# Small tiles of a two-block transformer kernel moved into its pool of constants; scratch of the squares in bfloat16

## The chip, the core and the metric

The kernel runs on one core of one Trainium2 chip, in one launch. The metric is the device time in microseconds (us). A profile is one execution of its own, taken by the hardware profiler; its span runs from the first to the last instruction.

## What is computed

Two transformer blocks act on x of 256 tokens by 1024 features, all in float32:

```
def first_block(x, ...):
    h = _swiglu(_rms_norm(x, ffn1_pre_norm), ffn1_w_in, ffn1_w_out)          # 1024 -> 2 x 2816 -> 1024
    x = x + 0.5 * _rms_norm(h, ffn1_post_norm)
    m = _token_mixing(_rms_norm(x, mix_pre_norm), w_mix_in, ...)             # retention + neighbourhood attention
    x = x + _rms_norm(m, mix_post_norm)
    h = _swiglu(_rms_norm(x, ffn2_pre_norm), ffn2_w_in, ffn2_w_out)
    return x + 0.5 * _rms_norm(h, ffn2_post_norm)

def second_block(x, c, ...):
    mod = silu(c) @ ada_w + ada_b                                            # 2 x 6 x 1024 modulations
    for i in range(2):
        h = x * (1 + scale1) + shift1
        y = moba_attention(h, ...) if i == 0 else diff_attention(h, ...)
        x = layer_norm(sqrt(2) * x + (1 + gate1) * y, ln_g[i, 0], ln_b[i, 0])
        h = x * (1 + scale2) + shift2
        y = square(relu(h @ mlp_w_up[i])) @ mlp_w_down[i]                    # 1024 -> 4096 -> 1024
        x = layer_norm(sqrt(2) * x + (1 + gate2) * y, ln_g[i, 1], ln_b[i, 1])
    return x
```

## The kernel before

**Precision.** Every large product is made of three matmuls in the type fp32r. A weight tile `raw` (128 x 1024, float32) is rounded by ScalarE to `wh` (L115), and VectorE subtracts to get the rest `wl` (L93). Activations are kept the same way as a high and a low part, side by side in one tile (`XX`, `H`, `Y`, `N`). A product is high by high, low by high and high by low. In `mmA` (512 columns) the activation is the stationary operand and the weight moves; in `mmB` (256 columns) the weight is stationary and `XX` moves. This text calls the three matmuls of one call of `mmA` or `mmB` a triple. In the profile's names the moving operand comes first: `acc<-wh,H` moves `wh` past a stationary slice of `H`.

```
    def mmA(o, wh, wl, x, s, e):
        mm(o, x[:, 0], wh, s, False)
        mm(o, x[:, 0], wl, False, False)
        mm(o, x[:, 1], wh, False, e)
```

**Stages.** The first SwiGLU (`swiglu`, 11 slices of 256 hidden features), mixing, the second SwiGLU, then twice an attention and an MLP (`mlp`, 16 slices). `XX` holds the normalised, transposed input of a stage. `H` (four to five buffers) holds a slice of the hidden layer, and `down` and `down_tail` multiply it by the second weight matrix: 8 triples a slice. `Y` holds the merged heads: in mixing it is multiplied by `w_ret_out` (`yr`, 32 triples) and `w_mix_out` (`acc`, 32), in each attention by its output matrix (`oacc`, 32). `N` holds the heads of the neighbourhood attention (`yn`, 16 triples).

**Order of the work.** The order is written out by hand: `tick` brings in weight pieces up to a look-ahead (rings of 6 `raw` buffers and 8 of `wh` and `wl`) and runs side tasks. The modulations `ada` are summed on VectorE into `adacc` (L335, L338), split into three bfloat16 parts by ScalarE and GpSimd (L348 to L354) and multiplied on TensorE at set places.

**Where tiles lie.** A pool lays its tiles one behind the other in each partition, in the order of first use, each rounded up to a multiple of 32 bytes. The pools stand in the order const, wts, big, work, and behind them the pools of the stage at hand (hid, mix, att0, att1, ada, late). Tiles of a few bytes a partition (`s`, `r`, `sa`, `bs`, `mv` and the like: sums of squares, their roots, means) are in work, and in mix and att0/att1 (`nmx`, `m3`, `mx`, `ss`, `rs` and the like). The const pool has an odd number of blocks of 32 bytes behind `small`, and so has the work pool with its 29 small blocks. Adding up gives these starts, in bytes of the partition:

| tile | pool | start before | modulo 64 |
|---|---|---|---|
| `raw`, `wh`, `wl` | wts | 24128, 48704, 81472 and multiples of 4096 on | 0 |
| `X`, `XX`, `N` and `v`, `adacc`, `T` and `vt` | big | 114240, 122432, 138816, 147008, 151104 | 0 |
| `junk`, `a`, `b`, `q`, `hf` and the like (512 columns) | work | 159360, 161792 and multiples of 2048 on | 0 |
| `H` | hid | 180704 and multiples of 4096 on | 32 |
| `Y` | mix, att0, att1 | 176608, 186848 | 32 |
| `nv`, `bias`, `cosr`, `sinr`, `R` | mix | 192992 to 211424 | 32 |
| `q`, `k` of the attentions | att0, att1 | 203232 to 209376 | 32 |
| `ada0` to `ada2`, `grow`, `prow`, `lng`, `lnb` | ada, late, hid | 170464 to 192992 | 32 |
| `rq`, `rk`, `dec`, `nP`, `nT`, `P`, `T`, `o` | mix, att0, att1 | 211712 to 228096 | 0 |
| `identb`, `cmaskb`; `sm`, `adb`, `mod`, `csil` | const | 21888, 22144; 22432 to 23712 | 0; 32 |

The slices that TensorE loads start at multiples of 512 bytes within `XX`, `N`, `Y`, `H`, `wh` and `wl`.

The change touches the body of `block_kernel`, the helpers `rpow`, `rcol` and `squares`, the classes `PostRms`, `PostLn` and `Rms`, `log_sigmoid`, and the allocations in `mixing` and `attention`; all matmuls are recorded at L201 (`mm`).

Of the kernel before, what the change touches and what calls it, by code (L numbers as in the profile page):

```python
# [9 lines left out]
F32 = mybir.dt.float32  # L10
F32R = mybir.dt.float32r
BF16 = mybir.dt.bfloat16
AF = mybir.ActivationFunctionType
# [158 lines left out]
def block_kernel(ctx, tc, A, out):  # L172
    nc = tc.nc
    V, SC, PE, GP = nc.vector, nc.scalar, nc.tensor, nc.gpsimd

    const = ctx.enter_context(tc.tile_pool(name="const", bufs=1))
    wpool = ctx.enter_context(tc.tile_pool(name="wts", bufs=1))
    big = ctx.enter_context(tc.tile_pool(name="big", bufs=1))
    work = ctx.enter_context(tc.tile_pool(name="work", bufs=1))
# [45 lines left out]

    ident = cst[:, C_ID:C_ID + 128]
    identb = const.tile([128, 128], BF16, name="identb")
    cmaskb = const.tile([128, 128], BF16, name="cmaskb")
    small = const.tile([128, 4], F32, name="small")
    ones, mhalf, onesb = small[:, 0:1], small[:, 1:3], small[:, 3:4].bitcast(BF16)[:, 0:1]  # L230
# [316 lines left out]


    def rpow(s):
        r = work.tile([128, 2], F32, name="r", bufs=6)[:, 0:s.shape[1]]  # L550
        GP.tensor_tensor(r, s, mhalf[:, 0:s.shape[1]], OP.pow)
        return r

    def rcol(p, c, n, eps):
        s = work.tile([128, 2], F32, name="s", bufs=4)[:, 0:p.shape[1]]
        V.tensor_scalar(s, p, c / n, c * eps, op0=OP.mult, op1=OP.add)
        return rpow(s)

# [20 lines left out]

    def squares(s, src):  # L580

        SC.activation(work.tile([128, 512], F32, name="junk"), src, AF.Square, accum_out=s)

    def turn_of(src, a, c, alloc=gu):

# [24 lines left out]
    class PostRms:  # L610
# [2 lines left out]

        def __init__(self, accs, gain, coef, eps):
            self.accs, self.gain, self.coef, self.eps = accs, gain, coef, eps
            self.s = work.tile([128, 2, 2], F32, name="sa", bufs=2)
            self.m = {}

        def bank(self, t, f, ahead=nothing):
# [13 lines left out]
    class PostLn:  # L633
# [3 lines left out]
        def __init__(self, accs, gate):  # L637
            self.accs, self.gate = accs, gate
            self.v = big.tile([128, 2, D], F32, name="v", tag="P2")
            self.s = work.tile([128, 2, 2, 6], F32, name="bs")  # L640
            self.mv = work.tile([128, 2, 2], F32, name="mv", bufs=2)

        def bank(self, t, f, ahead=nothing):
            ahead(3)
            v = half(self.v[:, t], f)
            V.tensor_tensor(v, self.accs[t][f], half(self.gate, f), OP.mult)  # L646
            V.scalar_tensor_tensor(v, half(X[:, t], f), ALPHA, v, op0=OP.mult, op1=OP.add)  # L647
            V.bn_stats(self.s[:, t, f], v)  # L648
            if f:
                V.bn_aggr(self.mv[:, t], self.s[:, t].rearrange("p f s -> p (f s)"))  # L650
                e = work.tile([128, 1], F32, name="ve", bufs=2)
                V.tensor_scalar(e, self.mv[:, t, 1:2], 0.0, LN_EPS, op0=OP.max, op1=OP.add)  # L652
                self.norm(t, self.mv[:, t, 0:1], rpow(e))

        def norm(self, t, mu, r):
            n = work.tile([128, 1], F32, name="nm", bufs=2)
            V.scalar_tensor_tensor(n, mu, -1.0, r, op0=OP.mult, op1=OP.mult)
            SC.activation(half(self.v[:, t], 0), half(self.v[:, t], 0), AF.Identity, scale=r, bias=n)
            V.tensor_scalar(half(self.v[:, t], 1), half(self.v[:, t], 1), mu, r, op0=OP.subtract, op1=OP.mult)
# [22 lines left out]
    class Rms:  # L682


        def __init__(self):
            self.s = work.tile([128, 2, 2], F32, name="s2", bufs=2)

        def token(self, t):
            for f in range(2):
                squares(self.s[:, t, f:f + 1], half(X[:, t], f))  # L690

        def close(self, c=1.0):
            s = work.tile([128, 2], F32, name="s3", bufs=2)
            V.tensor_tensor(s, self.s[:, :, 0], self.s[:, :, 1], OP.add)
            self.r = rcol(s, c, D, RMS_EPS)

# [103 lines left out]

    def log_sigmoid():
        x = bro[:, 0:8]
        a = work.tile([128, 8], F32, name="ls_a")
        e = work.tile([128, 8], F32, name="ls_e")
        s = work.tile([128, 8], F32, name="ls_s")
        z = work.tile([128, 8], F32, name="ls_z")
        V.scalar_tensor_tensor(a, x, -1.0, x, op0=OP.mult, op1=OP.max)
        yield 1
        SC.activation(e, a, AF.Exp, scale=-1.0)
        yield 1  # L810
        V.tensor_scalar(s, e, 2.0, None, op0=OP.add)
        V.reciprocal(s, s)
        V.tensor_tensor(s, s, e, OP.mult)
        V.tensor_tensor(z, s, s, OP.mult)
        V.memset(a, 1.0 / 21)
        for i in range(9, -1, -1):
            V.tensor_tensor(a, a, z, OP.mult)
            V.tensor_scalar(a, a, 1.0 / (2 * i + 1), None, op0=OP.add)
# [110 lines left out]
    def mixing(mid):  # L929
        with tc.tile_pool(name="mix", bufs=1) as mp:  # L930
# [21 lines left out]
            cosr = mp.tile([128, S], F32, name="cosr")  # L952
            sinr = mp.tile([128, S], F32, name="sinr")
            R = mp.tile([128, S], F32, name="R")
            rh = mp.tile([128, 2], F32, name="rh")
            sgs = {}
            vdone, nvdone = set(), set()

# [10 lines left out]
            def ret_head(h, q, k):  # L969
                hc = h % 2  # L970
                df, e = w2("df"), w2("de")
                GP.iota(two(df), pattern=[[-128, 2], [1, S]], base=0, channel_multiplier=-1,
                        allow_small_or_imprecise_dtypes=True)
                V.tensor_scalar(e, df, lgd[:, h:h + 1], None, op0=OP.mult)
                V.scalar_tensor_tensor(e, df, lgd[:, 4 + h:5 + h], e, op0=OP.mult, op1=OP.min)
                dec = m2("dec")
                SC.activation(dec, e, AF.Exp)
                yield 1
                p = acc("rs")
                for m in range(2):  # L980
                    mm(two(p)[:, m], two(k)[:, hc, m * 128:(m + 1) * 128], two(q)[:, hc], m == 0, True)
                V.scalar_tensor_tensor(dec, p, 128.0 ** -0.5, dec, op0=OP.mult, op1=OP.mult)
                yield 2
                while h not in vdone:
                    yield 1
                p = acc("ry")
                s = mp.tile([128, 2], F32, name="rys", bufs=2)
                for t in range(2):
                    for m in range(2):
                        mm(two(p)[:, t], two(dec)[:, m, t * 128:(t + 1) * 128], rv[:, m, h * 256:(h + 1) * 256],  # L990
                           t == 0 and m == 0, m == 1)
                sq = w2("rsq")
                for t in range(2):
                    SC.activation(two(sq)[:, t], two(p)[:, t], AF.Square, accum_out=s[:, t:t + 1])
                yield 1
                r = rcol(s, 4.0, 256, RMS_EPS)
                yield 1
                V.tensor_tensor(r, r, rms.r, OP.mult)
                while h not in sgs:
                    yield 1  # L1000
                g = sgs.pop(h)
                y = m2("ry")
                for t in range(2):
                    V.scalar_tensor_tensor(two(y)[:, t], two(p)[:, t], r[:, t:t + 1], g[t], op0=OP.mult, op1=OP.mult)
                yield 1
                for v in range(2):
                    for t in range(2):
                        PE.transpose(two(p)[:, v, t * 128:(t + 1) * 128], two(y)[:, t, v * 128:(v + 1) * 128], ident)
                split(Y[:, 2 * h:2 * h + 2, 0], Y[:, 2 * h:2 * h + 2, 1], two(p))

            def na_pair(j, q, k):
                cc = j % 2
                P = [m2("nP"), m2("nP")]
                ps = [acc("ns"), acc("ns")]
                mx = mp.tile([128, 4], F32, name="nmx", bufs=2)
                ss = mp.tile([128, 4], F32, name="nss", bufs=2)
                for c in range(2):
                    for a in range(2):
                        hs = slice(64 * a, 64 * a + 64)
# [1 line left out]
                for a in range(2):  # L1021
                    p = ps[a]
# [192 lines left out]
    def attention(l, turn, after, mid):  # L1215
        with tc.tile_pool(name=f"att{l}", bufs=1) as mp:
# [12 lines left out]

            def pair(j, q, k):  # L1230
                cc = j % 2
                m3 = mp.tile([128, 2, 3], F32, name="m3", bufs=2)
                mx = mp.tile([128, 2, 2], F32, name="mx", bufs=3)
                ss = mp.tile([128, 2, 2], F32, name="ss", bufs=4)
                yield from room(2)
                ps = [acc("as"), acc("as")]
                live[0] += 2
# [20 lines left out]
                if l == 0:  # L1258
                    V.reciprocal(ss, ss)
                else:  # L1260
                    rs = mp.tile([128, 2], F32, name="rs", bufs=4)
                    lr = mp.tile([128, 2], F32, name="lr", bufs=2)
                    V.reciprocal(lr, ss[:, :, 1])
                    V.reciprocal(rs, ss[:, :, 0])
                    V.scalar_tensor_tensor(lr, lr, lam[:, 1:2], ss[:, :, 0], op0=OP.mult, op1=OP.mult)
# [37 lines left out]
                                    two(p)[:, :, 0:128].rearrange("p c (a d) -> p c a d", a=2),  # L1303
                                    ss[:, :, :, None].to_broadcast([128, 2, 2, 64]), OP.mult)
                else:
                    sa = mp.tile([128, 2], F32, name="sa", bufs=2)
                    for c in range(2):
                        SC.activation(two(o)[:, c], two(p)[:, c, 0:128], AF.Square, scale=rs[:, c:c + 1],
                                      accum_out=sa[:, c:c + 1])
# [174 lines left out]
```

## Time and profile before

| | |
|---|---|
| median of 3 runs | 1317.36 us (1317.07 to 1321.57) |
| the profiled execution, its own time | 1319.84 us |
| its span | 1318.0 us |
| TensorE busy | 1258.1 us, 95% |
| VectorE, ScalarE, GpSimd busy | 932.2, 642.8, 94.6 us |
| mean granted TensorE clock | 0.983 of 2.4 GHz |
| read from HBM | 269.37 MB |

The time of a matmul in the profile is from its first column in to its last result out, and matmuls overlap: what one costs in a row of them is the distance from its start to the next one's start, which the timeline shows.

### The profile page before, as it was taken

How to read it: one execution, taken by the hardware profiler on the slowest of the kernel's cores; microseconds unless marked ns; L12 is line 12 of the kernel's file. 1: busy time of each engine (PE TensorE's matmuls, PEld its weight loads, DVE VectorE, ACT ScalarE, POOL GpSimd, SP SyncE). 2: the span in 40 equal slices, each digit the busy share in tenths (PEclk: the TensorE clock that was granted, in tenths of full speed). 3: DMA queues.
4: the chain of work that ended last, by engine and by line, in shares of the span. 5: the costliest groups of instructions: out<-in, count | busy, mean ns of one | idle time of the engine just before them, and what ended most of it. 6: DMA issues, size and time to landing. Idle time of an engine off the chain costs nothing. (4 is left out here: it accounts for less than half of the span.)

```text
span 1318.0 us, 18965 instructions
## 1 busy us (share of the span) xinstructions
PE 1258.1 (95%) x7217; PEld 1073.1 (81%) x7222; DVE 932.2 (71%) x1276; ACT 642.8 (49%) x1032; POOL 94.6 (7%) x69
## 2 busy tenths in 40 slices
PE   9999899999999999999999999999899889999996
PEld 7877677888888878778789978988878777899885
DVE  5687576888676677667577667768677976775655
ACT  6543355545454454445455544435444544643540
POOL 0010010222000001001000000101100001000100
PEclk9999999999999999999999999999999999999998
DMA  9778687866576477878554336877665333576650
GB/s 305 258 250 278 212 258 168 261 212 193 190 223 205 145 249 236 290 258 266 171 181 137 112 118 215 266 256 262 221 231 176 113 109 126 175 249 222 223 192 32
DMA packets 167884, 271.68 MB, mean 206 GB/s; under 512 B 15888, under 2 KB 119664, under 8 KB 167792
## 3 DMA queue, kind: packets, MB, share of 16 engines
q1 hardware_dynamic: 161328, 268.36, 62.9%
q10 hardware_dynamic: 6464, 2.10, 1.0%
q8 instruction: 57, 0.93, 0.3%
q14 instruction: 35, 0.29, 0.1%
HBM read 269.37 MB, written 1.05 MB: 205 GB/s over the span
## 5 line engine op out<-in xcount | busy, mean ns | idle before, releaser
L93 DVE TENSOR_TENSOR wl<-raw,wh 128x1024 fp32r<-128x1024 f32 x392 | 487.9, 1273 | 58.2 <-ACT wh L115 57.0
L115 ACT ACTIVATE wh<-raw 128x1024 fp32r<-128x1024 f32 x392 | 399.7, 1055 | 161.7 <-issue 29.2
L201 PE MATMUL acc<-wh,H 128*128 128x512 f32 x864 | 286.5, 399 | 1.5 <-ACT wh L115 1.5
L201 PE MATMUL g<-wh,XX 128*128 128x512 f32 x832 | 268.3, 397 | 2.0 <-DVE XX L596 1.6
L201 PEld LDWEIGHTS acc<-wh,H 128*128 128x128 f32 x864 | 163.7, 189 | 43.2 <-issue 3.0
L201 PEld LDWEIGHTS g<-wh,XX 128*128 128x128 f32 x832 | 158.4, 190 | 37.5 <-DVE XX L596 2.0
L201 PE MATMUL acc<-wl,H 128*128 128x512 f32 x432 | 173.2, 401 | 1.5 <-DVE wl L93 1.5
L201 PE MATMUL g<-wl,XX 128*128 128x512 f32 x416 | 164.6, 396 | 5.2 <-DVE wl L93 5.2
L201 PE MATMUL u<-XX,wh 128*128 128x256 f32 x896 | 163.9, 284 | 1.5 <-ACT wh L115 1.5
L201 PEld LDWEIGHTS u<-XX,wh 128*128 128x128 f32 x896 | 142.2, 193 | 4.2 <-ACT wh L115 1.9
L201 PE MATMUL u<-XX,wl 128*128 128x256 f32 x448 | 127.5, 285 | 2.9 <-DVE wl L93 2.9
L338 DVE SCALAR_TENSOR_TENSOR adacc<-raw,csil,adacc 128x1024 f32<-128x1024 f32 x84 | 107.4, 1279 | 0.8
L201 PEld LDWEIGHTS g<-wl,XX 128*128 128x128 f32 x416 | 79.3, 191 | 23.2 <-DVE wl L93 7.1
L201 PEld LDWEIGHTS acc<-wl,H 128*128 128x128 f32 x432 | 82.0, 190 | 19.2 <-DVE wl L93 2.1
L201 PEld LDWEIGHTS u<-XX,wl 128*128 128x128 f32 x448 | 86.5, 193 | 3.3 <-DVE wl L93 3.3
L774 ACT ACTIVATE q<-u 128x512 f32<-128x512 f32 x28 | 16.8, 600 | 122.0 <-PE u L201 122.0
L775 DVE TENSOR_TENSOR q<-q,u 128x512 f32<-128x512 f32 x28 | 19.2, 686 | 80.0 <-ACT q L774 79.9
L711 ACT ACTIVATE a<-g,r 128x256 f32<-128x256 f32 x44 | 20.4, 474 | 93.4 <-PE g L201 93.4
L350 POOL TENSOR_TENSOR adacc<-adacc,ada 128x1024 f32<-128x1024 f32 x12 | 25.8, 2152 | 551.6 <-ACT ada L348 494.1
L713 DVE SCALAR_TENSOR_TENSOR b<-g,r,a 128x256 f32<-128x256 f32 x44 | 20.7, 481 | 58.0 <-ACT a L711 57.9
L201 PE MATMUL v<-wh,XX 128*128 128x256 f32 (+1 forms) x192 | 49.4, 344 | 5.1 <-DVE XX L606 5.1
L201 PE MATMUL q<-XX,wh 128*128 128x256 f32 x256 | 47.4, 286 | 0.0
(289 smaller groups left out, 1818.4 us busy)
## 6 DMA issues: line engine op xcount, KB each, us to landing
raw<-in_ada_w_dram SPq DMA_DIRECT2D x96, 512.0 KB, 5.2
raw<-in_ffn_w_in_dram SPq DMA_DIRECT2D x176, 256.0 KB, 5.0
raw<-in_mlp_w_up_dram SPq DMA_DIRECT2D x64, 512.0 KB, 4.8
raw<-in_mlp_w_down_dram SPq DMA_DIRECT2D x64, 512.0 KB, 4.8
raw<-in_w_mix_in_dram SPq DMA_DIRECT2D x52, 512.0 KB, 4.8
raw<-in_ffn_w_out_dram SPq DMA_DIRECT2D x44, 512.0 KB, 5.7
raw<-in_moba_w_in_dram SPq DMA_DIRECT2D x24, 512.0 KB, 4.7
raw<-in_diff_w_in_dram SPq DMA_DIRECT2D x24, 512.0 KB, 4.8
```

The lines of the kernel that those rows point to most:

```text
L93: self.nc.vector.tensor_tensor(wl, raw, wh.bitcast(F32), OP.subtract)
L115: nc.scalar.activation(wh, raw, AF.Copy)
L201: PE.matmul(o, l, r, start=start, stop=stop, skip_group_check=True)
L338: V.scalar_tensor_tensor(t, w, csil[:, kb:kb + 1], t, op0=OP.mult, op1=OP.add)
L350: GP.tensor_tensor(t, t, parts[0], OP.subtract)
L711: SC.activation(two(a)[:, t], ps[t][:, 0:256], AF.Silu, scale=r[0][:, t:t + 1])
L713: V.scalar_tensor_tensor(two(b)[:, t], ps[t][:, 256:512], r[0][:, t:t + 1], two(a)[:, t], op0=OP.mult, op1=OP.mult)
L774: SC.activation(q, p, AF.Relu)
L775: V.tensor_tensor(q, q, p, OP.mult)
```

## The change

Three things:

- All the small tiles of work, mix, att0 and att1 are allocated in the const pool, with the names and numbers of buffers that they had (one of the two that were named `sa` is now `sq`). No large tile stands behind a small one any more.
- A tile of 32 bytes, `even`, which nothing reads or writes, stands in the const pool before `cmaskb`.
- The scratch of the squares, `junk` (512 columns, never read), becomes bfloat16: 1024 bytes in place of 2048.

The built program has the same instructions in the same order on every engine, with the same waits; only addresses differ, and the type of `junk`. Every tile of 256 bytes or more then starts at a multiple of 64 but `cmaskb`, which goes from 0 to 32 modulo 64: `raw`, `wh` and `wl` at 25856, 50432 and 83200, `XX` at 124160, `N` at 140544, `Y` at 176384 and 186624, `H` at 180480 and multiples of 4096 on, the `q` and `k` of the attentions at 203008 to 209152. All of these are multiples of 128 as well; `XX`, `N` and the weights were at 64 modulo 128 before.

```diff
     identb = const.tile([128, 128], BF16, name="identb")
+    const.tile([128, 8], F32, name="even")
     cmaskb = const.tile([128, 128], BF16, name="cmaskb")
...
     def rpow(s):
-        r = work.tile([128, 2], F32, name="r", bufs=6)[:, 0:s.shape[1]]
+        r = const.tile([128, 2], F32, name="r", bufs=6)[:, 0:s.shape[1]]
         GP.tensor_tensor(r, s, mhalf[:, 0:s.shape[1]], OP.pow)
         return r
...
     def squares(s, src):
-        SC.activation(work.tile([128, 512], F32, name="junk"), src, AF.Square, accum_out=s)
+        SC.activation(work.tile([128, 512], BF16, name="junk"), src, AF.Square, accum_out=s)
...
-            self.s = work.tile([128, 2, 2, 6], F32, name="bs")
-            self.mv = work.tile([128, 2, 2], F32, name="mv", bufs=2)
+            self.s = const.tile([128, 2, 2, 6], F32, name="bs")
+            self.mv = const.tile([128, 2, 2], F32, name="mv", bufs=2)
...
-                m3 = mp.tile([128, 2, 3], F32, name="m3", bufs=2)
-                mx = mp.tile([128, 2, 2], F32, name="mx", bufs=3)
-                ss = mp.tile([128, 2, 2], F32, name="ss", bufs=4)
+                m3 = const.tile([128, 2, 3], F32, name="m3", bufs=2)
+                mx = const.tile([128, 2, 2], F32, name="mx", bufs=3)
+                ss = const.tile([128, 2, 2], F32, name="ss", bufs=4)
...
-                    sa = mp.tile([128, 2], F32, name="sa", bufs=2)
+                    sa = const.tile([128, 2], F32, name="sq", bufs=2)
```

The hunks left out do the same (`work.tile` or `mp.tile` to `const.tile`) for `s`, `sa`, `ve`, `nm`, `s2`, `s3`, `ls_a`, `ls_e`, `ls_s`, `ls_z`, `rh`, `rys`, `nmx`, `nss`, `rs` and `lr`.

## Rows read from the trace of the kernel before

**Rows 1.** The page: busy time by engine.
```profile
PE 1258.1 (95%) x7217; PEld 1073.1 (81%) x7222; DVE 932.2 (71%) x1276; ACT 642.8 (49%) x1032; POOL 94.6 (7%) x69
```

**Rows 2.** Windows: from:to, length, busy (count) of PE, PEld, DVE, ACT, POOL; clock, DMA, GB/s.
```profile
89.00:180.00 91.00, 80.12 (x376) 62.97 (x375) 62.00 (x74) 35.07 (x43) 9.87 (x4) 0.96 0.76 248
...
810.00:940.00 130.00, 124.93 (x819) 111.53 (x818) 96.77 (x96) 55.95 (x67) 12.26 (x5) 0.99 0.77 256
...
1155.00:1287.00 132.00, 131.95 (x843) 118.82 (x844) 81.47 (x82) 59.58 (x71) 5.20 (x2) 1.00 0.66 216
```

**Rows 3.** Timeline of PE, stage `yn`, stationary `N`: start us, us, form, count.
```profile
407.46 0.39 PE L201 MATMUL yn<-wl,N 128*128 128x512 f32 x1
...
409.50 0.39 PE L201 MATMUL yn<-wl,N 128*128 128x512 f32 x1
```

**Rows 4.** Timeline of PE, stage `yr`, stationary `Y`.
```profile
354.35 0.40 PE L201 MATMUL yr<-wl,Y 128*128 128x512 f32 x1
...
356.45 0.40 PE L201 MATMUL yr<-wl,Y 128*128 128x512 f32 x1
```

**Rows 5.** Timeline of PE, second MLP, stationary `H`.
```profile
1205.09 0.40 PE L201 MATMUL acc<-wl,H 128*128 128x512 f32 x1
...
1209.99 0.40 PE L201 MATMUL acc<-wl,H 128*128 128x512 f32 x1
```

**Rows 6.** By tile (`N`, `Y`, `H`): count, ns min/median/max, first to last start us; forms.
```profile
L201 PEld LDWEIGHTS yn<-wh,N x32: 187/188/188, 407.0 to 430.2; 128*128 128x128 f32 x32
...
L201 PEld LDWEIGHTS yr<-wh,Y x64: 186/188/190, 353.9 to 395.9; 128*128 128x128 f32 x64
L201 PE MATMUL oacc<-wl,Y x64: 392/392/403, 755.1 to 1117.8; 128*128 128x512 f32 x64
L201 PE MATMUL yr<-wl,Y x32: 392/399/399, 354.4 to 395.9; 128*128 128x512 f32 x32
L201 PE MATMUL acc<-wl,Y x32: 392/392/399, 430.9 to 454.3; 128*128 128x512 f32 x32
...
L201 PE MATMUL acc<-wl,H x432: 388/399/628, 43.9 to 1307.5; 128*128 128x512 f32 x144
```

**Rows 7.** Groups of PE in 89 to 180, then in 810 to 940: busy, mean ns, waits.
```profile
L201 PE MATMUL acc<-wl,H 128*128 128x512 f32 x32 | 13.3, 416 | 0.8 <-DVE wl L93 0.8
...
L201 PE MATMUL acc<-wl,H 128*128 128x512 f32 x88 | 35.2, 400 | 0.7 <-DVE wl L93 0.7
```

**Rows 8.** Waits of PE over the span: us in total, times, longest.
```profile
PE g L201 <- POOL ada L354: 5.6, 2, 2.9
...
PE g L201 <- DVE wl L93: 5.2, 5, 1.9
```

**Rows 9.** By tile, columns as in rows 6: moving `nv` and `vt`; VectorE and ScalarE.
```profile
L201 PE MATMUL no<-nv,nT x64: 217/275/275, 333.5 to 376.3; 128*128 128x64 f32 x64
...
L201 PE MATMUL ao<-vt,T x144: 217/275/377, 701.4 to 1098.8; 128*128 128x64 f32 x96, 128*128 128x128 f32 x48
...
L546 DVE TENSOR_TENSOR H<-q,H x28: 677/684/2630, 810.4 to 1289.3; 128x512 fp32r<-128x512 f32 x28
...
L607 DVE TENSOR_TENSOR XX<-hf,XX x16: 691/693/695, 656.3 to 1129.4; 128x512 fp32r<-128x512 f32 x16
...
L348 ACT ACTIVATE ada<-adacc x12: 1047/1057/1059, 85.5 to 1221.4; 128x1024 bf16<-128x1024 f32 x12
...
L115 ACT ACTIVATE wh<-raw x392: 1037/1052/1112, 16.9 to 1287.2; 128x1024 fp32r<-128x1024 f32 x196
```

**Rows 10.** Timeline of PE: `ry` moves `rv` past `dec` (8 matmuls), to the next matmul's start.
```profile
258.47 1.89 PE L201 MATMUL ry<-rv,dec 128*128 128x256 f32 x8
260.19 1.03 PE L201 MATMUL rs<-rq,rk 128*128 128x256 f32 x4
```

**Rows 11.** Timeline of PE, after a wait at the start of the second SwiGLU.
```profile
463.70 1.18 PE L201 MATMUL g<-wh,XX 128*128 128x512 f32 x2 [1.61 <-DVE XX L596]
...
468.09 0.40 PE L201 MATMUL g<-wl,XX 128*128 128x512 f32 x1
```

More of the change, by code (lines that the diff above doesn't have):

```diff
@@ L554, in rcol @@
     def rcol(p, c, n, eps):
-        s = work.tile([128, 2], F32, name="s", bufs=4)[:, 0:p.shape[1]]
+        s = const.tile([128, 2], F32, name="s", bufs=4)[:, 0:p.shape[1]]
         V.tensor_scalar(s, p, c / n, c * eps, op0=OP.mult, op1=OP.add)
@@ L615, in __init__ @@
             self.accs, self.gain, self.coef, self.eps = accs, gain, coef, eps
-            self.s = work.tile([128, 2, 2], F32, name="sa", bufs=2)
+            self.s = const.tile([128, 2, 2], F32, name="sa", bufs=2)
             self.m = {}
@@ L650, in bank @@
                 V.bn_aggr(self.mv[:, t], self.s[:, t].rearrange("p f s -> p (f s)"))
-                e = work.tile([128, 1], F32, name="ve", bufs=2)
+                e = const.tile([128, 1], F32, name="ve", bufs=2)
                 V.tensor_scalar(e, self.mv[:, t, 1:2], 0.0, LN_EPS, op0=OP.max, op1=OP.add)
@@ L655, in norm @@
         def norm(self, t, mu, r):
-            n = work.tile([128, 1], F32, name="nm", bufs=2)
+            n = const.tile([128, 1], F32, name="nm", bufs=2)
             V.scalar_tensor_tensor(n, mu, -1.0, r, op0=OP.mult, op1=OP.mult)
@@ L685, in __init__ @@
         def __init__(self):
-            self.s = work.tile([128, 2, 2], F32, name="s2", bufs=2)
+            self.s = const.tile([128, 2, 2], F32, name="s2", bufs=2)
         def token(self, t):
@@ L692, in close @@
         def close(self, c=1.0):
-            s = work.tile([128, 2], F32, name="s3", bufs=2)
+            s = const.tile([128, 2], F32, name="s3", bufs=2)
             V.tensor_tensor(s, self.s[:, :, 0], self.s[:, :, 1], OP.add)
@@ L802, in log_sigmoid @@
         x = bro[:, 0:8]
[L803 to L806, printed above, removed]
+        a = const.tile([128, 8], F32, name="ls_a")
+        e = const.tile([128, 8], F32, name="ls_e")
+        s = const.tile([128, 8], F32, name="ls_s")
+        z = const.tile([128, 8], F32, name="ls_z")
         V.scalar_tensor_tensor(a, x, -1.0, x, op0=OP.mult, op1=OP.max)
@@ L954, in mixing @@
             R = mp.tile([128, S], F32, name="R")
-            rh = mp.tile([128, 2], F32, name="rh")
+            rh = const.tile([128, 2], F32, name="rh")
             sgs = {}
@@ L986, in ret_head @@
                 p = acc("ry")
-                s = mp.tile([128, 2], F32, name="rys", bufs=2)
+                s = const.tile([128, 2], F32, name="rys", bufs=2)
                 for t in range(2):
@@ L1014, in na_pair @@
                 ps = [acc("ns"), acc("ns")]
-                mx = mp.tile([128, 4], F32, name="nmx", bufs=2)
-                ss = mp.tile([128, 4], F32, name="nss", bufs=2)
+                mx = const.tile([128, 4], F32, name="nmx", bufs=2)
+                ss = const.tile([128, 4], F32, name="nss", bufs=2)
                 for c in range(2):
@@ L1260, in pair @@
                 else:
-                    rs = mp.tile([128, 2], F32, name="rs", bufs=4)
-                    lr = mp.tile([128, 2], F32, name="lr", bufs=2)
+                    rs = const.tile([128, 2], F32, name="rs", bufs=4)
+                    lr = const.tile([128, 2], F32, name="lr", bufs=2)
                     V.reciprocal(lr, ss[:, :, 1])
```

## The prediction

> **What bounds the kernel now.** I read the page first, then windows by stage, then the matmuls one by one. TensorE is busy 95% of the span, VectorE 71%, ScalarE 49% [rows 1]. In the second MLP, 132 us, TensorE is idle for 0.05 us while VectorE is busy 81.47 of 132 [rows 2]: what a matmul takes there is paid in full. In the first SwiGLU (89 to 180 us) and the first MLP (810 to 940) TensorE idles for 10.9 and 5.1 us, waiting for weights or for the modulations [rows 2, 8]. So the question is what the change does to the distance between matmuls, and how much of that the waits swallow.
>
> That distance is not the same for all. With `N` stationary, three triples go from 407.46 to 409.50: 0.680 us a triple [rows 3]. With `Y` stationary, in the same `mmA`, with the same 512 columns of `wh` and `wl` moving and a tile of the same inner layout, three triples go from 354.35 to 356.45: 0.700 us [rows 4]. With `H`, seven triples take 4.90 us: 0.700 [rows 5]. `N` starts at 0 modulo 64; `Y` and `H` start at 32. The durations say the same: median 392 to 399 ns a matmul with `Y` and `H` [rows 6].
>
> **The change part by part.** No instruction is added, removed or moved, and no wait. Only addresses change.
>
> *Stationary slices of `H` and `Y`, from 32 to 0 modulo 64.* I take it that they then go as `N` does: 0.020 us less a triple. Triples are the counts of the middle matmul: 432 with `H`, and 64, 32 and 32 with `Y` [rows 6], 560 in all. 560 x 0.020 = 11.2 us, if TensorE is never made to wait instead.
>
> *What the waits swallow.* A wait whose end is set by a DMA, VectorE or GpSimd eats what was saved since the stage began. Four places:
> - 89 to 180: 32 triples with `H` [rows 7], 0.64 us, in front of 10.9 us of waits, of which `wl` is 5.2 and GpSimd's `ada` up to 2.9 [rows 8].
> - The second SwiGLU waits once more for `ada` [rows 8]. Taken as the first: 0.64 us at risk.
> - 810 to 940: 88 triples [rows 7], 1.76 us, in front of 5.1 us of waits [rows 2].
> - The last output matrix (`oacc`) is interleaved with the last heads of that attention: at most its 32 triples, 0.64 us.
>
> So 3.7 us are at risk, and 7.5 us are left if all of it goes. But VectorE and ScalarE wait for TensorE in each slice too, and are free for weights earlier when TensorE is; VectorE is busy 96.77 of 130 us even at 810 to 940 [rows 2], so supply is not full. I take half of the risk as lost: 11.2 - 1.85 = 9.35 us saved, with 7.5 and 11.2 as ends.
>
> *Other operands that move from 32 to 0.* Moving ones: `nv` (at 32) and `vt` (at 0) move the same 64 columns in the same 275 ns median [rows 9], so moving operands cost nothing either way. VectorE reads `q` at 0 with `H` at 32 in 684 ns, and `hf` with `XX`, both at 0, in 693 [rows 9]: nothing to gain; at worst 9 ns more on the 28 instructions for `H`, 0.25 us on an engine that is 71% busy, and covered by that. GpSimd on `adacc` and `ada` has no row with both at 0: between a gain of the whole 5.6 us that TensorE waits for it and a loss of as much again; the VectorE rows are nearest, so 0. The `q` of the attentions and the bfloat16 `ada` are stationary as well, some 320 short matmuls, whose loads may gain up to the 7 ns a matmul that `Y` shows, 2.2 us; I take 0, since I see no row of them at the other start.
>
> *`cmaskb` and `small`, from 0 to 32.* On TensorE both only move; to the other engines `small` is an operand of one or two columns. By the `nv` row, 0.
>
> *Small tiles in const.* Same numbers of buffers, same waits: 0. *`junk` in bfloat16:* 24 squares on ScalarE. A bfloat16 output of 1024 columns takes 1057 ns, an fp32r one 1052 [rows 9]; nothing reads `junk`: 0.
>
> *All other tiles, from 64 to 0 modulo 128.* No fp32r slice in the trace has that start. Bounds: 0, and the second rival below. I take 0: `Y` at 96 and `N` at 64 modulo 128 differ in the half of a block of 64 where they start, and that is what goes.
>
> **Sum.** The profiled execution took 1319.84 us, of which the span is 1318.0; it would be 1310.5. It lies 2.5 us above the median of the runs shown. Against that median: 1317.36 - 9.35 = **1308.0 us**, 0.7% faster. About 0.5% (6.6 us) is what a measurement of this kernel can tell from no change.
>
> **The rivals.**
>
> *The start is not the cause.* `Y` and `H` also lie higher in the partition (from 176384 on) than `N` and `XX` (below 147008), and after the change they still do. Then the slow triples stay, and the time is 1317.4 us. For it: the weight loads themselves take 188 ns with `N` and with `Y` [rows 6], so the view of loads shows no trace of a start. Against it: `rv` is moved past `dec`, which lies at 216576, in 0.215 us for 256 columns (8 matmuls from 258.47 to 260.19 [rows 10]), with no sign of a slow region; but `dec` is plain float32. The Trainium skill, page "Advanced Engine Details and Errata", section "SBUF Cachelines", gives lines of 16 bytes and full speed for accesses within a line. By that rule a start at 32 modulo 64 is as good as one at 0, the change does nothing, and the time is 1317.4 us. The difference between rows 3 and 4 is what it would have to leave unexplained.
>
> *Every stationary slice gains.* If what matters is 128 or more, the weights and `XX` gain too. The row to go by is `dec`, a multiple of 128: 256 columns of plain float32 in 0.215 us, where an fp32r matmul of 512 columns takes 0.680 / 3 = 0.227. That is 0.011 us for some 6,000 fp32r matmuls of the 7217 [rows 1], 66 us on top of the rest at most; VectorE's 932 us would not forbid it. The time would be 1242 us at least, anywhere up to 1300. Against it: `H` and `N` differ already, so the smaller block decides.
>
> *Slower: new waits that drop TensorE's clock.* After the wait of 1.61 us at 463.70 TensorE's granted clock is at its lower level, 1.2 in place of 2.4 GHz, for a stretch: the 11 distances from 463.70 to 468.09 take 4.39 us, where 11 x 0.227 = 2.5 us would do; 1.9 us lost, beside the wait [rows 11]. If TensorE outruns the weights in the second half of each MLP and SwiGLU, waits that are now too short turn into such waits. Each gives back 1.9 us, so five new ones eat the 9.35 us, and nine would make it slower by 0.5%: 1325 us. For it: DMA share 0.76 and 0.77 in the two stretches that wait already [rows 2]. Against it: in the second MLP VectorE has 50 us to spare and there are no waits at all to grow [rows 2]; the saving in a slice of the MLP is 8 x 0.02 = 0.16 us, a tenth of such a wait.
>
> **How the numbers follow.** The forecast has 0.74, the start not being the cause 0.13, every slice gaining 0.07, slower 0.06. The forecast's own range is 1317.4 - 11.2 - 3.8 = 1302.4 (two drops of the clock fewer) to 1317.4 - 7.5 + 3.8 = 1313.7 (two more). To leave out no more than 2 in 10 it must reach the first rival, 1317.4: the range is 1303 to 1317.5. Faster by over 0.5% (below 1310.8): 0.65 of the forecast's 0.74 and the 0.07 of the second rival, 0.72. Slower by over 0.5%: 0.05. The rest, 0.23, is within 0.5%.
>
> **What would show it.** Triples with `H` and `Y` should stand 0.680 us apart, as with `N`, and their matmuls' medians fall to 389 ns; those with `N`, `XX` and stationary weights should stay. Durations on VectorE, ScalarE and GpSimd should stay. The waits for `wl` and `ada` in 89 to 180 and 810 to 940 should grow by some 2 us together. I am wrong if `H` and `Y` stay at 0.700 (first rival), if `N` and `XX` go below 0.680 (second), or if the triples shrink and the clock's mean falls below 0.983 (third).

## The result and the profile after

| | before | after |
|---|---|---|
| median of 13 runs each | 1319.75 us (1317.07 to 1326.69) | 1313.86 us (1309.81 to 1317.80) |
| ratio after to before | | 0.9945, 95% interval 0.9926 to 0.9963 |
| the profiled execution, its own time; its span | 1319.84; 1318.0 us | 1311.53; 1309.7 us |

The change is 0.55% faster, some 7.3 us; the two profiled executions differ by 8.3. The page's busy time of the changed kernel, the windows that answer to [rows 2], and two more (the second SwiGLU from 493, the first MLP from 805):

```profile
PE 1245.8 (95%) x7217; PEld 1071.6 (82%) x7222; DVE 933.1 (71%) x1276; ACT 642.2 (49%) x1032; POOL 95.4 (7%) x69
```
```profile
89.00:180.00 91.00, 79.80 (x376) 63.00 (x375) 62.09 (x74) 35.26 (x43) 9.91 (x5) 0.96 0.76 247
810.00:940.00 130.00, 124.54 (x826) 113.16 (x825) 92.11 (x91) 54.24 (x66) 12.40 (x5) 0.97 0.77 256
1155.00:1287.00 132.00, 131.95 (x831) 119.24 (x831) 80.08 (x80) 58.52 (x70) 5.19 (x2) 1.00 0.62 202
...
493.00:651.00 158.00, 155.11 (x724) 126.99 (x724) 112.59 (x113) 75.64 (x96) 15.36 (x7) 1.00 0.76 254
...
805.00:977.00 172.00, 163.90 (x1018) 146.24 (x1017) 126.17 (x133) 76.31 (x95) 16.16 (x7) 0.97 0.74 248
```

TensorE is busy 12.3 us less than in [rows 1], VectorE and ScalarE as long as before. The stretches with waits have about as much idle time of TensorE as before: 11.2 and 5.5 us, against 10.9 and 5.1.

The timeline of TensorE in the changed kernel (start us, us, form, count, idle time ahead): `Y` and `N` stationary, `mmB` (`u`), two places in the first MLP, `H` stationary:

```profile
354.33 0.39 PE L201 MATMUL yr<-wl,Y 128*128 128x512 f32 x1
...
356.37 0.39 PE L201 MATMUL yr<-wl,Y 128*128 128x512 f32 x1
...
406.89 0.39 PE L201 MATMUL yn<-wl,N 128*128 128x512 f32 x1
...
408.93 0.39 PE L201 MATMUL yn<-wl,N 128*128 128x512 f32 x1
...
879.87 0.28 PE L201 MATMUL u<-XX,wl 128*128 128x256 f32 x1
...
882.39 0.28 PE L201 MATMUL u<-XX,wl 128*128 128x256 f32 x1
...
926.04 0.39 PE L201 MATMUL acc<-wh,H 128*128 128x512 f32 x1
...
938.30 0.40 PE L201 MATMUL acc<-wh,H 128*128 128x512 f32 x1
...
973.40 1.97 PE L590 MATMUL xt<-cst,v 128*128 128x128 f32 x8 [2.59 <-ACT v L659]
...
976.95 0.39 PE L201 MATMUL acc<-wh,H 128*128 128x512 f32 x1
...
1197.94 0.40 PE L201 MATMUL acc<-wl,H 128*128 128x512 f32 x1
...
1199.32 0.39 PE L201 MATMUL acc<-wl,H 128*128 128x512 f32 x1
...
1202.72 0.39 PE L201 MATMUL acc<-wl,H 128*128 128x512 f32 x1
```

Three triples with `Y` take 2.04 us, 0.680 each, where they took 2.10 [rows 4]; five with `H` take 3.40, again 0.680, where they had 0.700 [rows 5]. `N` stays at 0.680 [rows 3]. The rows from 879.87 to 976.95 are used below.

Not every triple takes the step. The first two triples of that slice of `H`, right behind `mmB`, take 1.38 us (1197.94 to 1199.32), where [rows 5] shows a whole slice of before with 0.700 in every triple, the first ones too. In most slices of the SwiGLUs the last four triples, which follow transposes, stand 0.690 to 0.705 apart. Over all neighbouring matmuls (distances over 300 ns left out) the mean distance falls from 233.5 to 228.1 ns with `H` and from 233.5 to 227.7 with `Y`. For 432 and 128 triples that is some 9.2 us, not 11.2.

The view by tile of the changed kernel shows the step too (count, ns min/median/max):

```profile
L201 PE MATMUL oacc<-wl,Y x64: 387/389/398, 748.9 to 1111.2; 128*128 128x512 f32 x64
L201 PE MATMUL yr<-wl,Y x32: 389/389/398, 354.3 to 395.3; 128*128 128x512 f32 x32
...
L201 PE MATMUL acc<-wl,H x432: 387/389/628, 44.4 to 1299.0; 128*128 128x512 f32 x144
```

All medians are 389 ns, from 392 to 399 [rows 6]. The waits of TensorE in the changed kernel, against [rows 8]:

```profile
PE g L201 <- POOL ada L355: 5.6, 2, 2.9
PE g L201 <- DVE wl L93: 5.5, 5, 1.9
```

The same to 0.3 us. Where the 11.2 us of the forecast's sum went is told by stage. The last column is the difference of the two traces between the starts of the last middle matmul of each stage:

| stage | triples with `H`, `Y` | at 0.020 us | measured |
|---|---|---|---|
| until the first product | | 0 | +0.55 |
| first SwiGLU | 88 | -1.76 | -1.03 |
| mixing | 64 | -1.28 | -0.71 |
| second SwiGLU | 88 | -1.76 | -3.53 |
| first attention | 32 | -0.64 | -1.84 |
| first MLP | 128 | -2.56 | +1.33 |
| second attention | 32 | -0.64 | -1.33 |
| second MLP | 128 | -2.56 | -1.96 |
| rest | | 0 | +0.13 |
| sum | 560 | -11.2 | -8.39 |

The two stages that are furthest off, the second SwiGLU and the first MLP, have another granted clock. Two windows of before, for the two of after that begin at 493 and 805:

```profile
494.00:656.00 162.00, 158.89 (x725) 128.27 (x725) 113.00 (x114) 76.35 (x97) 14.74 (x7) 0.99 0.76 249
...
811.00:983.00 172.00, 164.84 (x1023) 144.73 (x1024) 125.67 (x133) 76.34 (x94) 16.03 (x7) 0.99 0.74 247
```

The second SwiGLU goes from 0.99 to 1.00, the first MLP from 0.99 to 0.97. (The second attention has 0.97 in both traces; why it gained 1.33 us is not shown.) Two places of the MLP show how. In the one, between two slices of `H`, TensorE waits for `wh` and `wl`; in the other, at the end, for ScalarE's `v`. The timeline of before there:

```profile
933.55 0.39 PE L201 MATMUL acc<-wh,H 128*128 128x512 f32 x1
...
944.94 0.39 PE L201 MATMUL acc<-wh,H 128*128 128x512 f32 x1
...
980.09 1.09 PE L589 MATMUL xt<-cst,v 128*128 128x128 f32 x8 [1.99 <-ACT v L658]
...
982.18 0.39 PE L201 MATMUL acc<-wh,H 128*128 128x512 f32 x1
```

At the end TensorE of the changed kernel arrives earlier, waits 2.59 us in place of 1.99, and its clock is then at the lower of its two levels, 1.2 GHz: the eight `xt` take 1.97 us in place of 1.09, and from the first of them to the same `acc` product it is 3.55 us (973.40 to 976.95) in place of 2.09 (980.09 to 982.18). The place costs 0.60 + 1.46 = 2.06 us. The earlier place costs another 0.87 us: 12.26 (926.04 to 938.30) in place of 11.39 (933.55 to 944.94), with a granted clock of 0.86 in the 25 us around it, from 0.93. Together that is more than the stage gained from its triples. How much such waits cost changes from one execution to the next: another one of the same kernel (the run `after_again` below) has 0.977 over its whole span, and 1317.3 us.

### The profile page after: what moved, and what is told of

Read it like the earlier page. It is cut to its first block, busy times and chain, and to the rows that moved or that the text cites. A ratio compares the mean times of both kernels' runs of the same rounds, so it can differ in the third digit from the quotient of the medians.

```text
span 1309.7 us, 18965 instructions
## 1 busy us (share of the span) xinstructions
PE 1245.8 (95%) x7217; PEld 1071.6 (82%) x7222; DVE 933.1 (71%) x1276; ACT 642.2 (49%) x1032; POOL 95.4 (7%) x69
## 5 line engine op out<-in xcount | busy, mean ns | idle before, releaser
L201 PE MATMUL acc<-wh,H 128*128 128x512 f32 x864 | 283.1, 396 | 1.5 <-ACT wh L115 1.5
L201 PE MATMUL acc<-wl,H 128*128 128x512 f32 x432 | 169.6, 393 | 1.6 <-DVE wl L93 1.6
```

Source lines behind the costliest of these rows:

```text
L201: PE.matmul(o, l, r, start=start, stop=stop, skip_group_check=True)
```

## The experiments

**What was in question.** The forecast took the start of the stationary tile modulo 64 as the cause. The rival that the runs brought up: what counts is the *distance*, the start of the next stationary slice minus the start of the operand that is moving, modulo some power of two. In the kernel before, weights and `N` and `XX` are at distance 0, `H` and `Y` at 416 modulo 512; in the changed kernel all are at 0. The start modulo 64 and the distance change together there, so the change itself can't tell them apart. (Slices of one tile start at multiples of 512 from one another, so no run tells the next slice from the one in use.) Below, a spacing is the median distance from a matmul's start to the next one's. In a fast triple the three are alike; in a slow one they differ (mostly 231, 232 and 238 ns with `H` before), so a median of 232 stands for a triple of 0.700 us.

**`pad_work`: only `H`, `Y` and what lies behind them moved by 32 bytes.** Before, with a tile of 32 bytes at the end of work:

```diff
+        work.tile([128, 8], F32, name="pad")
```

> The kernel before with one unused tile of 32 bytes in the work pool: H, Y, nv, prow and the like move by 32 bytes to 0 modulo 64; the small tiles, junk in float32 and all of const, raw, wh, wl, X, XX, N stay where they were; the plain float32 tiles rq, rk, dec, nP, nT, P, T, o of mixing and attention go from 0 to 32. Theory (the start modulo 64 of the stationary slice): triples with H and Y fall from 0.700 to 0.680 us, and the time is that of the change, a ratio of about 0.9945 to before, unless the plain float32 stationary tiles pay at 32: then some 200 short matmuls lose up to 7 ns each, 1.4 us. Rival (the place in the partition): H and Y lie 32 bytes from where they lay, so 0.700 and a ratio of 1.000. Rival (small tiles in const, or junk in bfloat16, bring part of the gain): a ratio between 0.9945 and 1.

Measured: 1318.03 us, ratio 0.9964 (0.9949 to 0.9979). Only part of the gain, as neither the theory nor the place in the partition has it. Its timeline:

```profile
1191.83 0.39 PE L201 MATMUL acc<-wl,H 128*128 128x512 f32 x1
...
1195.26 0.39 PE L201 MATMUL acc<-wl,H 128*128 128x512 f32 x1
```

Five triples in 3.43 us are 0.686: `H` starts at 0 modulo 64 and is still not as fast as `N`. The distance is now 448 modulo 512, spacing 229 ns (1593 pairs with `H` or `Y`), between the 232 of 416 and the 227 of 0. The plain float32 tiles behind, moved from 0 to 32, kept their times.

**`no_even`: the changed kernel without `even`.** Every large tile then starts at 32 modulo 64, with the distances unchanged.

```diff
-    const.tile([128, 8], F32, name="even")
```

> The change without the unused tile even: everything behind small is 32 bytes earlier, so that all large tiles, raw, wh, wl, X, XX and N too, lie at 32 modulo 64. Theory: triples with N and XX rise to 0.700 us as well, and the triples with stationary weights (832 of 256 columns, 0.360 now) to 0.380: 2,032 triples x 0.020 = 40.6 us over the change, less what waits swallow: 1345 to 1355 us, a ratio of 1.019 to 1.027 to before. Rival (place): nothing moves by more than 32 bytes, so the time of before or of the change, 0.994 to 1.000. Rival (moving operands or VectorE pay too): more than 1.03.

Measured: 1315.21 us, ratio 0.9946 (0.9927 to 0.9966). Its timeline:

```profile
1203.79 0.39 PE L201 MATMUL acc<-wl,H 128*128 128x512 f32 x1
...
1207.19 0.39 PE L201 MATMUL acc<-wl,H 128*128 128x512 f32 x1
```

Five triples in 3.40 us, 0.680, with `H` at 32 modulo 64. The expected rise to 1.019 or more did not come, and the forecast's cause falls: the start modulo 64 does nothing, and `even` isn't needed.

**`weights32`: the weights moved against everything else.** `no_even`, with 32 bytes at the end of the pool of the weights: `raw`, `wh`, `wl` stay at 32 modulo 64, `XX`, `N`, `H`, `Y` go to 0.

```diff
+        wpool.tile([128, 8], F32, name="pad")
```

> The change with raw, wh and wl alone at 32 modulo 64 (even left out, and 32 bytes put behind the weights), so X, XX, N, H and Y at 0. It parts the roles: wh and wl move in 1,200 triples (mmA) and are stationary in 832 (mmB). Theory (stationary alone): mmA triples stay at 0.680, mmB triples go from 0.360 to 0.380 us: 832 x 0.020 = 16.6 us over the change, a ratio of about 1.005 to 1.008 to before. Rival (moving operands pay as well): mmA triples rise above 0.680 too, up to 24 us more, a ratio of 1.02 or above. VectorE's 1217 ns and ScalarE's 1052 ns on raw and wh stay in both, unless they read by blocks of 64 too.

Measured: 1321.2 us, ratio 0.9987 (0.9974 to 1.0001). The gain is gone. By tile, `XX` and `H`, and the timeline of `mmA` with `H`:

```profile
L201 PE MATMUL g<-wl,XX x416: 389/395/630, 8.4 to 641.0; 128*128 128x512 f32 x139
...
L201 PE MATMUL acc<-wl,H x432: 392/395/628, 43.9 to 1304.7; 128*128 128x512 f32 x144
```
```profile
1203.98 0.40 PE L201 MATMUL acc<-wl,H 128*128 128x512 f32 x1
...
1208.18 0.40 PE L201 MATMUL acc<-wl,H 128*128 128x512 f32 x1
```

Six triples in 4.20 us, 0.700. `XX`, that was always fast and now starts at 0 modulo 128, is slow too: 234 ns at distance 32 (the median of some 3,300 pairs of `mmA`). And `mmB`, where the weights are stationary and `XX` moves, became *faster*: 117 ns in place of 120 (2435 pairs). Against the changed kernel 560 triples with `XX` are slower and 832 of `mmB` faster, so the time is close to before. The small tiles lie in const here and `junk` is bfloat16, as in the change, and the triples with `H` are back at 0.700: neither brings the gain.

**`off_a`: `H` 16, `Y` 4 and `N` 48 bytes further on, in longer tiles.** The changed kernel with

```diff
-            H = hp.tile([128, 2, 2, S], F32R, name="H", bufs=4)
+            H = shifted(hp, 2, "H", 4, bufs=4)
```

where `shifted` gives a view from float 4 on in a tile that is 16 floats longer, and the like for `Y` (from 1) and `N` (from 12). The longer tiles put the buffers of `H` 64 bytes apart modulo 512.

> The change with H at 16, Y at 4 and N at 48 bytes modulo 64, each as a slice of a tile 64 bytes longer; XX and the weights at 0. Which starts pay? Theory of blocks of 64: any start off a multiple of 64 pays the same, so 0.700 us a triple for all three. Rival, lines of 16 bytes: H and N start on a line and stay at 0.680, Y pays. Rival, a price that grows with the distance from 64: H about 0.690, Y 0.683, N 0.690 or 0.710.

Measured: one run, 1317.3 us. `Y` at distance 68: 233 ns; `N` at 48: 234, for the first time slow; `XX`, untouched, 227. The four buffers of `H` stand at 80, 144, 208 and 272 and differ: 231, 227, 233, 233. In the second MLP, one slice at 208 and one at 144:

```profile
1214.33 0.40 PE L201 MATMUL acc<-wl,H 128*128 128x512 f32 x1
...
1219.20 0.40 PE L201 MATMUL acc<-wl,H 128*128 128x512 f32 x1
...
1225.65 0.39 PE L201 MATMUL acc<-wl,H 128*128 128x512 f32 x1
...
1230.41 0.39 PE L201 MATMUL acc<-wl,H 128*128 128x512 f32 x1
```

4.87 us for seven triples (0.696), then 4.76 (0.680). None of the three expectations has that: it is no matter of "aligned or not".

**`scan_h` and `scan_xx`: many distances in one kernel.** The changed kernel with its own offset for each of the 54 slices of `H`, and again with one for `XX` in each of the seven stages:

```diff
+    OFF = ([4 * i for i in (1, 2, 3, 5, 6, 7, 9, 11, 13, 14, 15)], [512 - 4 * i for i in (1, 2, 3, 5, 6, 7, 9, 11, 13, 14, 15)],
+           [32 * i for i in range(16)], [32 * i + 16 for i in range(16)])
...
+    xx_offs = [o // 4 for o in (480, 16, 256, 64, 128, 48, 288)]
```

> The change with every one of the 54 slices of H shifted within a longer tile by its own number of bytes: in the MLPs by 0, 32, ..., 480 and 16, 48, ..., 496, in the two SwiGLUs by 4 to 60 bytes and by 4 to 60 bytes short of 512 (not by multiples of 16). The start modulo 64 alone has fallen: with all tiles at 32 modulo 64 the triples stood 0.680 us apart. New theory (distance): what counts is the distance of the stationary slice's start from that of the moving tile, which is 0 modulo 512 in the change and in the version with all at 32. Then a slice shifted by 0 has 0.680, one by 32 has 0.700, one by 448 has 0.687 and one by 416 has 0.700, as measured so far, and slices that are 256 apart need not agree. Rival (blocks of 64 for the distance): 64, 128, ... are all 0.680 to 0.690, all others 0.700. If some distance gives less than 0.680, a version faster than both kernels exists.

> The change with XX shifted by another number of bytes in each stage: first SwiGLU 480, mixing 16, second SwiGLU 256, first attention 64, first MLP 128, second attention 48, second MLP 288. It scans the distance for the triples with stationary weights and moving XX (0.360 us at distance 0, 0.351 when the weights lay 32 bytes below XX modulo 512). Theory (distance, weights minus XX, modulo 512): the triples of mmB differ from stage to stage between 0.35 and 0.37 us, with the same value for the same distance; with XX shifted by 32 the value was 0.351. Rival (mmB gains from the weights' own start at 32 modulo 64): the weights start at 0 here, so 0.360 in all stages. The mmA triples of the second SwiGLU (256) tell whether the period is 256 (0.680) or longer.

Measured: one run each, 1317.12 and 1316.89 us. The spacing of `mmA` by distance modulo 512 in `scan_h` (some 22 pairs each, ns):

```
  0: 227   32: 234   64: 235   96: 234  128: 232  160: 232  192: 229  224: 234
 16: 234   48: 233   80: 231  112: 233  144: 227  176: 229  208: 233  240: 227
256: 228  288: 235  320: 236  352: 234  384: 232  416: 231  448: 233  480: 234
272: 233  304: 233  336: 230  368: 233  400: 227  432: 229  464: 234  496: 229
```

The first two lines come back in the last two, 256 bytes on, within 2 ns but at 192: a period of 256 fits. Each value is one slice, and in some the triples differ: 240 has 0.680 throughout, 496 has 0.684 to 0.698. (The offsets that are no multiples of 16 have medians from 227, at 12, 28 and 500, to 235.) A slice of the first MLP, at 320, and one of the second, at 144:

```profile
925.74 0.40 PE L201 MATMUL acc<-wl,H 128*128 128x512 f32 x1
...
930.64 0.39 PE L201 MATMUL acc<-wl,H 128*128 128x512 f32 x1
...
1191.74 0.39 PE L201 MATMUL acc<-wl,H 128*128 128x512 f32 x1
...
1196.50 0.39 PE L201 MATMUL acc<-wl,H 128*128 128x512 f32 x1
```

Seven triples in 4.90 and in 4.76 us. With `XX` in `scan_xx` the same distances gave the same: 227 at 256 (514 pairs), 234 at 480 (514), 236 at 64, 235 at 288. The 256 in a whole SwiGLU is the best evidence of the period. Its timeline, first SwiGLU at 480, second at 256:

```profile
67.99 0.40 PE L201 MATMUL g<-wl,XX 128*128 128x512 f32 x1
...
69.39 0.40 PE L201 MATMUL g<-wl,XX 128*128 128x512 f32 x1
...
502.83 0.39 PE L201 MATMUL g<-wl,XX 128*128 128x512 f32 x1
...
509.63 0.39 PE L201 MATMUL g<-wl,XX 128*128 128x512 f32 x1
```

Two triples in 1.40, then ten in 6.80 us. For `mmB` it is the other way round: 120 ns at distance 0 and 117 to 118 at 224, 448, 464 and 496; at 384 it is 120. So the zero that is best for `mmA` is the worst, or nearly, for `mmB`.

**`all144`, `all240`, `xx32`, `after_again`: can both be had?** Distances that were fast for `mmA` in `scan_h` and aren't 0. In the first two, `XX`, `H`, `Y`, `N` all begin 144 or 240 bytes further on; in the third only `XX` does, by 32 in the attentions and MLPs, where most matmuls with `XX` are `mmB`; the fourth is the changed kernel once more. The view of the first (`all240` has 60 for 36; both are without `even`), and the offsets of the third, one for each stage:

```diff
+    def shifted(pool, n, name, **kw):
+        t = pool.tile([128, 2 * n * S + 64], F32R, name=name, **kw)
+        return t[:, 36:36 + 2 * n * S].rearrange("p (k i s) -> p k i s", i=2, s=S)
```
```diff
+    xx_offs = [o // 4 for o in (0, 0, 0, 32, 32, 32, 32)]
```

> XX, H, Y and N all begin 144 bytes further on than in the changed kernel, inside tiles that are 256 bytes longer; the weights lie at 224 modulo 256, and so would XX, H, Y and N without the 144. Theory (the distance from the moving operand's start to the next stationary slice's start, modulo 256, sets the spacing): mmA has distance 144, which showed 227 ns on two slices of H, so every mmA triple with XX, H, Y and N stays at 0.680 us although no stationary slice starts at a multiple of 64. mmB has the distance 112, which no run has shown: between 116 ns (the least seen at any distance) and 122 ns. With 2496 matmuls in mmB that is between 10 us less and 5 us more of TensorE's time than the changed kernel; at half of it in the span, a ratio to before of 0.991 to 0.997. Rival (the zero distance alone is good for long runs, the 144 on two slices was chance): mmA 229 to 234 ns, and a ratio of 1.000 to 1.008.

> As the run with 144 bytes, but 240. Theory: mmA has the distance 240, which showed 227 ns on one slice of H, and mmB 16, which no run has shown: mmA triples at 0.680 us, mmB between 116 and 122 ns a matmul, a ratio to before of 0.991 to 0.997. Rival (zero alone is good): mmA at 229 to 234 ns, as at 496 and 16, a ratio of 1.000 to 1.008.

> The changed kernel, with XX 32 bytes further on in the two attentions and the two MLPs alone; H, Y, N and the weights keep distance 0 modulo 256. Theory of the distance: mmB in these four stages, some 2,150 matmuls, goes from 120 to 117 ns (6.4 us less), some 190 matmuls of mmA with XX there from 227 to 234 ns (1.3 us more): TensorE busy 5 us less than in the changed kernel. If the waits take a third, as they did with H and Y (12.3 us less busy, 8.4 us less span), 3.4 us faster than the changed kernel, a ratio to before of 0.992. Rival (in these stages the waits take it all, since the first MLP and the attentions wait for weights): the spacings change as said, the time is that of the changed kernel, 0.9945.

> The changed kernel once more, on the same chip as the three others, as the bound to beat: a ratio of 0.9945, between 0.9926 and 0.9963 as measured before, and triples of 0.680 us with H, Y, N and XX, mmB at 120 ns.

| | median us | ratio to before | TensorE busy us | `mmA` ns | `mmB` ns |
|---|---|---|---|---|---|
| `all144` | 1323.08 | 1.0016 (0.9998 to 1.0034) | 1255.5 | 232 | 118 |
| `all240` | 1309.95 | 0.9919 (0.9892 to 0.9945) | 1245.9 | 227 | 117 |
| `xx32` | 1308.66 | 0.9917 (0.9892 to 0.9941) | 1244.1 | 227 (190 at 235) | 117 (mixing 120) |
| `after_again` | 1314.25 | 0.9943 (0.9924 to 0.9963) | 1253.7 | 227 | 120 |

(The busy times are of one execution each; that of `after_again` had the lowest clock, 0.977.) `all240` and `xx32` did what the distance says. `all144` did not: 144 gave a median of 232 ns or so in all stages, with `XX` as with `H`, where two slices had given 227. The expectation was a miss there. And the median hides that single slices are fast. Two neighbours in the second MLP of `all144`, both behind `mmB`:

```profile
1194.60 0.40 PE L201 MATMUL acc<-wl,H 128*128 128x512 f32 x1
...
1199.37 0.39 PE L201 MATMUL acc<-wl,H 128*128 128x512 f32 x1
...
1205.65 0.39 PE L201 MATMUL acc<-wl,H 128*128 128x512 f32 x1
...
1210.55 0.40 PE L201 MATMUL acc<-wl,H 128*128 128x512 f32 x1
```

Seven triples in 4.77 us (0.681), then in 4.90 (0.700). Four of the 16 slices there are fast throughout, in turn with slow ones. Their buffers lie 4352 bytes apart, so their distances are the same modulo 256 and differ by 256 modulo 512; `scan_h` had 0.680 at both, 144 and 400. The rule "the distance modulo 256 sets the spacing" is not whole. The intervals of `after_again` and `xx32` overlap by a little.

**`xh144`: what 144 hangs on.** `XX` and `H` alone by 144, with all weights at multiples of 256 as in the scan:

> XX and H alone 144 bytes further on; Y, N and all weights at multiples of 256. In the run with 144 bytes everywhere the weights were at 224 modulo 256 and mmA took 232 ns; in the run with a start of its own for every slice of H the weights were at 0 modulo 256 and the two slices at 144 took 227. If the place of the weights themselves counts beside the distance, mmA with XX and H takes 227 ns here, as Y and N at distance 0 do. If the weights' place doesn't count and the 227 of those two slices came from what stood around them, it takes 232. mmB has the distance 112: 118 ns, as in the run with 144 bytes everywhere, or less.

Measured: one run, 1321.33 us; `mmA` with `H` and `XX` 232 ns, with `Y` (distance 0) 227, `mmB` 118. Its timeline:

```profile
1206.91 0.39 PE L201 MATMUL acc<-wl,H 128*128 128x512 f32 x1
...
1211.81 0.39 PE L201 MATMUL acc<-wl,H 128*128 128x512 f32 x1
```

Seven triples in 4.90 us. The weights' own place isn't it, though three slices of `H` (two in the first SwiGLU, one in the first MLP) have 0.680 here too. `off_a` gives a hint: there 272 gave 0.680 in the first slices of both SwiGLUs and 0.698 to 0.702 in seven of eight of the MLPs; 144 gave 0.680 in five of eight of the MLPs, and in the SwiGLUs 0.680 in the first half of a slice and 0.696 to 0.702 in the second, which follows transposes. So what ran just before a row of triples seems to count (`mmA` with `XX` or transposes in a SwiGLU, `mmB` in an MLP); but in `all144` neighbours differ behind the same `mmB`. What decides at distances other than 0 and 240 stays open.

**`xx240`: `XX` by 240 in all stages, the rest as in the change.**

```diff
-    XX = big.tile([128, KB, 2, S], F32R, name="XX")
+    XX = big.tile([128, KB * 2 * S + 64], F32R, name="XX")
+    XX = XX[:, 60:60 + KB * 2 * S].rearrange("p (k i s) -> p k i s", i=2, s=S)
```

> The changed kernel with XX 240 bytes further on in all stages; H, Y, N and the weights at multiples of 256. By the distance: mmB has 16 and takes 117 ns in all 2496, mmA with XX has 240 and stays at 227, mmA with H, Y and N at 0 stays at 227. TensorE is busy some 2 us less than with XX moved by 32 in four stages, since the mixing's mmB gains too (1.1 us) and the 190 of mmA don't lose 1.3 us; the ratio to before is then 0.990, between 0.988 and 0.993. If mmA with XX at 240 takes the 229 ns that some slices of H showed at 496, its 1680 lose 3.4 us and the ratio is 0.993.

Measured: 1307.25 us (1305.45 to 1307.83), ratio 0.9905 (0.9888 to 0.9921): below the interval of the change in both measurements of it (narrowly: 0.9921 against 0.9924 and 0.9926), so this version beats both kernels. `mmA` with `XX` stays at 227 ns, `mmB` takes 117 in all stages. The page's busy time, and the timeline of `mmB` in the first MLP:

```profile
PE 1239.4 (95%) x7217; PEld 1064.3 (82%) x7222; DVE 932.9 (72%) x1276; ACT 642.4 (49%) x1032; POOL 95.7 (7%) x69
```
```profile
879.82 0.28 PE L201 MATMUL u<-XX,wl 128*128 128x256 f32 x1
...
882.28 0.28 PE L201 MATMUL u<-XX,wl 128*128 128x256 f32 x1
```

Seven triples of `mmB` in 2.46 us, 0.351. In the changed kernel seven of them go from 879.87 to 882.39, 2.52 us, 0.360. Over 832 triples that is 7.5 us; 6.4 of it shows in the busy time (1245.8 to 1239.4).

## Why the prediction was right, and where its reason was wrong

- **What bounds the kernel: right.** TensorE's spacing was paid nearly in full. In the second MLP, where TensorE idles for 0.05 us of 132 as before, 1.96 of 2.56 us came through; over the whole span 8.4 of 11.2.
- **The size of the step: right in a running row, too big for the sum.** `H` and `Y` go from 0.700 to 0.680 us a triple, their medians to 389 ns; `N`, `XX` and stationary weights are unchanged, as forecast. But 560 x 0.020 counts every triple, and those right behind other matmuls stay above 0.680: the sum comes to some 9.2 us, not 11.2.
- **The cause, "from 32 to 0 modulo 64": wrong.** `no_even` has all tiles at 32 and is as fast as the change; `pad_work` has `H` and `Y` at 0 and comes only to 0.686; `weights32` makes the fast `XX` slow by moving the *weights*. What the change does is bring `H` and `Y` to distance 0 from the weights. `N` in [rows 3] was fast because it stood at distance 0, not for its start. The step that failed is "moving operands cost nothing either way", read from `nv` and `vt` with 64 columns: with 512 columns the place of the moving weights decides between 0.680 and 0.700. The comparison of `N` with `Y` was right, but two things differed between them, and the text named one. A look at the starts of the weights in the same table would have shown the other. That the forecast came out all the same is luck: this change brings `H` and `Y` both to start 0 and to distance 0, as `N` was, so the row of `N` gave the right price for the wrong reason.
- **The share that waits swallow: not in kind.** The forecast lost 1.85 us to waits for `wl` and `ada`, and expected these to grow by some 2 us. They grew by 0.4 (`g` 10.8 to 11.1, `u` for `wl` 2.9 to 3.0). Of the 2.8 us that are missing in the profile, 2.0 are the triples that did not take the step, and 0.55 is a later start. Then 2.93 are lost at the two places of the first MLP where TensorE waits and its clock is low, and about as much is made good, by the clock in the second SwiGLU and by the attentions.
- **The time itself.** 1308.0 was forecast and 1313.86 measured. Of these 5.9 us, 2.4 are the median of before, 1317.36 in three runs and 1319.75 in thirteen. The rest is the saving: 9.35 forecast, 8.3 between the profiled executions, 7.3 by the ratio, 5.9 between the medians. The term that was too big is the 11.2: with 9.2 in its place, the forecast's own loss of 1.85 leaves 7.35. That this meets the 7.3 is luck as well, since the loss was not in the waits that it named.
- **The rivals.** *The start is not the cause* was half right: it is not, but the triples shrank all the same. The Trainium skill, page "Advanced Engine Details and Errata", section "SBUF Cachelines", gives lines of 16 bytes. Both 0 and 32 are starts of such a line, and `no_even` agrees that the one is as good as the other (0.9946 against 0.9945). What the forecast drew from it, that the change then does nothing, is not borne out, since two operands' places count together. *Every slice gains* fell: 227 ns with `XX` stayed. *Slower by drops of the clock*: its mechanism is what the two places in the first MLP show, 2.06 us at one of them; elsewhere the clock fell less often than before, and its mean over the span is 0.984, from 0.983.
- **What was costed at nothing was nothing.** ScalarE and VectorE are busy as long as before, to 1 us, and `junk` and the moved small tiles show no cost.

## What to carry to other kernels

Where the same matmul has two spacings in one trace, list every address that differs between the two cases, of both operands, before naming a cause, and make one run that moves the other operand. For long rows of fp32r matmuls with a weight load each, these runs speak for starts of stationary slice and moving operand that are equal modulo 256 with 512 moving columns, and 16 bytes apart with 256 moving columns (128 apart, at 384, gained nothing); a view that begins some floats into a longer tile does it. Distances other than those measured must be tried in the place where they run, since 144 gave two answers. And look beside the median at the rows themselves: the gain of a row may not reach its first triples.

## What was not expected of the hardware

- The spacing of fp32r matmuls of 512 columns takes values from 227 ns (distance 0, and 240) to 236 (64, 320), and a period of 256 bytes in the distance between two operands fits, while the weight load itself shows a median of 188 ns with `H` at distance 0, 416 and 32 alike.
- With 256 columns and the roles exchanged, distance 0 is the slow case: 120 ns, against 117 at 16, 224 and 480.
- At 144 and 272 a row of triples keeps one of two spacings, 0.680 or 0.696 to 0.702 us, and neighbours at the same distance can differ. At distance 0 too the triples behind other matmuls start above 0.680. No run here shows why.
